# A list schedule that models the port of VectorE and GpSimd, with refitted durations and load queue

## The chip, the cores and the metric

The kernel runs on one core of one Trainium2 chip. The core has TensorE (matrix products, results in PSUM), VectorE, ScalarE and GpSimd (work on tiles in SBUF; VectorE and ScalarE also read PSUM) and SyncE, which issues the DMA transfers. In the profile these are PE, PEld (TensorE's weight loads), DVE, ACT, POOL and SP. The metric is device time in microseconds of one execution.

## The reference

Two layers of a block work on x of 1024 tokens by 1024 columns, in float32. Each layer normalises x, projects it to three mixers, joins their outputs, and runs a gated FFN of width 2816. The mixers are an attention over the 256 keys that an index score selects per query (`dsa`), a recurrent RWKV-7 mixer with eight heads, and an attention with compressed, selected and windowed keys (`nsa`).

```python
def reference(x, c, ...):
    for l in range(DEPTH):
        mod = jax.nn.silu(c) @ ada_w[l] + ada_b[l]
        sh1, sc1, g1, sh2, sc2, g2 = jnp.split(mod[:, None, :], 6, axis=-1)
        h = rms_norm(x, norm1_g[l]) * (1.0 + sc1) + sh1
        z = h @ w_in[l]
        za, zb, zc = split_cols(z, (sum(A_COLS), sum(B_COLS), sum(C_COLS)))
...
        mixed = jnp.concatenate([o_a, o_b, o_c], axis=-1) @ w_out[l]
        x = x + g1 * mixed
        h = rms_norm(x, norm2_g[l]) * (1.0 + sc2) + sh2
        gate, up = jnp.split(h @ ffn_wi[l], 2, axis=-1)
        x = x + g2 * ((jax.nn.silu(gate) * up) @ ffn_wo[l])
    return x
```

## The kernel before

Activations lie transposed, 128 features by 512 tokens, and the 1024 tokens are worked in two halves. A dense product (`dense`, output tile `mm`) splits weights and activations into a high and a low part and adds three products: high by high, high by low, low by high. Each weight tile of 128x512 (`wraw`) is loaded, its high part `whi` made by ScalarE and its low part `wlo` by GpSimd (`split`, called from `Feed.ahead`). `norm` and `rsqrt` make reciprocal roots with a chain of small VectorE instructions on 128x128 tiles (`nex` for the norms, `kex` for keys and queries, `ex` in RWKV, `rx`, `ru`, `ry` for narrow ones), then `cast` spreads them with matmuls (`rb`, `bc`). `attend` makes scores (`at`), masks and maxima on VectorE (`p`, `m`, `nb`), exponentials on ScalarE, scales `p` by `rs` on VectorE, transposes it on TensorE (`pt`), copies it with ScalarE (`pT`) and multiplies by the values (`po`). `topk` finds a threshold bit by bit: for each of 31 bits VectorE and ScalarE count (`junk`, `junka`, `tk_cn`), and three or four narrow VectorE instructions follow. `rw_unit` is the RWKV mixer of two heads (`am`, `A`, `TX`, `Tn`, `S`, `sh`, `sd`, `y`, `o`).

The order of all this is not written out by hand. It is made in three passes when the kernel is built.

1. `Weave.run` runs the generators of all streams (projections and FFN, attention, top-k, compression, RWKV, the modulation) in turns. It keeps a clock per engine from `cost_of` and `LAT` and takes the stream of best priority that is due and whose buffers fit. A first run finds how long each tile lives, a second one uses it. The result is a list of records (`Program.add`) with buffers given out; a record's number is its place in this list.
2. `Program.order` list-schedules the records. Each engine has a heap of records whose inputs are there. The engine that is free earliest takes its record of lowest number. It models TensorE as 4x4 cells so that narrow matmuls overlap, ScalarE's table loads, and loads as one wire of 390 GB/s that end 1.7 us after their bytes.
3. `Program.issue` emits the records sorted by their planned start. From there each engine's queue is in that order, and semaphores make it wait where an input is late.

Costs depend on the engine key (`PE`, `V`, `S`, `G`, `D` for loads), the operation and the width n. All instructions come out of one line of `issue`, so the profile shows L672 for nearly all; they are told apart by their tiles.

Of the kernel before, what the change touches and what calls it, by code (L numbers as in the profile page):

```python
# [18 lines left out]
AF = mybir.ActivationFunctionType  # L19
# [7 lines left out]
D = 1024  # L27
# [159 lines left out]
class Held:  # L187


    def __init__(self, weave, tag, key, make):  # L190
        self.weave, self.tag, self.key, self.make = weave, tag, key, make
        self.touches, self.end, self.got = 0, 0.0, None
# [8 lines left out]
    def __getattr__(self, name):  # L201
        return getattr(self.view(), name)
# [18 lines left out]
class Weave:  # L221
# [150 lines left out]
    def add(self, prio, gen, scope=None):  # L372
        c = self.cur
        c.children += 1
        self.live.append(Stream(prio, self.now(), len(self.live) + 1e-3, gen, scope or (c.scope, "child", c.children)))
# [37 lines left out]
    pass  # L413


LAT = {"PE": 0.17, "V": 0.1, "S": 0.1, "G": 0.1, "D": 0.0}


def cost_of(key, name, aps, kw):

    n = max(x.free_size() if callable(x.free_size) else x.free_size for x in aps[:2])
    psum = any(x.space == PSUM for x in aps[:3])
    acc = "accum_out" in kw
    if key == "V":
        if psum:
            return 0.1 + n / 860.0 + (0.1 if acc else 0.0)
        if name == "tensor_scalar":
            return 0.2 + n / 1250.0 + (0.2 if acc else 0.0)
        if name == "tensor_tensor_scan":
            return 1.25  # L430
        return 0.22 + n / 820.0
    if key == "S":
        return 0.18 + n / 1180.0 + (0.19 if acc else 0.0)
    if key == "G":
        return 0.12 + n / 417.0 if name == "tensor_tensor" else 0.1 + n / 1000.0
    a, b = aps[:2]
    plain = all(len(x.ap) <= 2 and x.ap[0][1] == 128 for x in (a, b))
    return 0.34 if plain else 0.59


class Timed:
# [5 lines left out]
    def __getattr__(self, name):  # L447
        f = getattr(self.eng, name)

        def call(*a, **k):  # L450
            a, k = [flat(x) for x in a], {n: flat(x) for n, x in k.items()}
            aps = [x for x in a + list(k.values()) if isinstance(x, bass.AP)]
            outs = [aps[0]] + ([k["accum_out"]] if "accum_out" in k else [])
            c = cost_of(self.key, name, aps, k)
            n = max(x.free_size() if callable(x.free_size) else x.free_size for x in aps[:2])
            self.weave.issue(self.key, 2.0 + n / 390.0 if self.key == "D" else c, aps, outs)
            if self.program is not None:
                self.program.add(self.key, name, a, k, aps, outs, c)
            else:
                f(*a, **k)  # L460

        return call
# [8 lines left out]


class Rec:
    __slots__ = ("key", "name", "a", "k", "cost", "deps", "n", "users", "pe", "func")


def spread(offset, dims, unit):
# [18 lines left out]
class Program:  # L496
# [29 lines left out]
            self.masks[key] = got  # L526
        return got

    def add(self, key, name, a, k, aps, outs, cost, pe=None):
        r = Rec()  # L530
        r.key, r.name, r.a, r.k, r.cost, r.pe = key, name, a, k, cost, pe
        r.n, r.deps, r.users = len(self.recs), set(), []
        r.func = a[2] if key == "S" and name == "activation" else None
        wrote = {id(x) for x in outs}
        for ap in aps:
            born = self.born.get(ap.tensor.name)
            if born is None:
                continue
            writes = id(ap) in wrote or (ap is aps[0])
            own = self.touched.setdefault(ap.tensor.name, ([], []))  # L540
            if born.pool == "ps":

                hit = False
                for e, w, eng in own[0]:
                    if w or writes:
                        r.deps.add(e)
                        hit = True
                if writes:
                    own[0].clear()
                if not hit and born.before is not None:  # L550
                    r.deps.update(born.before.recs)
                own[0].append((r.n, writes, key))
            else:
                p, m = self.region(ap, born)
                hit = False
# [12 lines left out]
                if writes:  # L568
                    assert not born.constant
                    own[0].append((r.n, p, m))  # L570
                elif born.pool != "const" or len(born.recs) < 400:
                    own[1].append((r.n, p, m))
                else:
                    born.constant = True
            born.recs.append(r.n)
        r.deps.discard(r.n)
        self.recs.append(r)

    def order(self):


        recs = self.recs
        missing = [len(r.deps) for r in recs]
        for r in recs:
            for d in r.deps:
                recs[d].users.append(r.n)
        free = {e: 0.0 for e in ("PE", "V", "S", "G", "D")}
        cells = [[0.0] * 4 for _ in range(4)]
        ready = {e: [] for e in free}
        coming = {e: [] for e in free}  # L590
        at = [0.0] * len(recs)
        wire, table = 0.0, None
        for r in recs:
            if not missing[r.n]:
                heapq.heappush(coming[r.key], (0.0, r.n))
        done, out = 0, []
        while done < len(recs):
            best = None
            for e in free:
                if ready[e]:  # L600
                    t = free[e]
                elif coming[e]:
                    t = max(free[e], coming[e][0][0])
                else:
                    continue
                if best is None or t < best[0]:
                    best = (t, e)
            t, e = best
            while coming[e] and coming[e][0][0] <= t:
                heapq.heappush(ready[e], heapq.heappop(coming[e])[1])  # L610
            n = heapq.heappop(ready[e])
            r = recs[n]
            if e == "PE":
                rows, cols, c = r.pe
                s = t
                for i in range(*rows):
                    for j in range(*cols):
                        s = max(s, cells[i][j])
                for i in range(*rows):
                    for j in range(*cols):  # L620
                        cells[i][j] = s + c
                free[e] = s + (c if rows[1] - rows[0] == 4 and cols[1] - cols[0] == 4 else 0.015)
                end = s + c
            elif e == "D":
                s = t
                free[e] = t + r.cost
                size = r.a[0].free_size() * r.a[0].partition_size() * 4
                wire = max(wire, free[e]) + size / 390e3
                end = wire + 1.7
            else:  # L630
                s, c = t, r.cost
                if r.func in (AF.Exp, AF.Silu) and r.func != table:
                    table, c = r.func, c + 1.28
                end = s + c
                free[e] = end - (0.05 if e == "V" else 0.02)
            out.append((s, n))
            done += 1
            for u in r.users:
                v = recs[u]
                at[u] = max(at[u], s + 0.001 if e == "PE" and v.key == "PE" else end + LAT[e])  # L640
                missing[u] -= 1
                if not missing[u]:
                    heapq.heappush(coming[v.key], (at[u], u))
        self.span = max(free.values())
        out.sort()
        return [recs[n] for _, n in out]

    def issue(self, tc, order, pools, inputs):
# [21 lines left out]
        with tc.manual_schedule():  # L670
            for r in order:
                getattr(engines[r.key], r.name)(*[real(x) for x in r.a], **{n: real(x) for n, x in r.k.items()})  # L672


def open_pools(ctx, tc):
# [1737 lines left out]
```

## Time and profile before

| | us |
|---|---|
| median of the runs shown | 3608.08 |
| lowest run | 3604.88 |
| the profiled execution's own time | 3599.41 |
| its span, first to last instruction | 3597.6 |
| mean granted clock of TensorE, share of full speed | 0.958 |

One run of the three shown took 11286.33 us; nothing here is compared with it. The profile page gives busy times of the whole span: PE 3318.0 us (92%), PEld 2503.0 (70%), DVE 2284.4 (63%), ACT 1820.8 (51%), POOL 1498.6 (42%). Busy is the time in which an engine executes at least one instruction; a busy VectorE or GpSimd instruction may be held up inside its own duration. `x232` counts instructions, `<-` stands between what is written and what is read.

### The profile page before, as it was taken

The page shows a single profiled execution, that of the slowest core. Times are in us where ns is not written, and L with a number is a line of the kernel's source. Part 1 is how long each engine was busy: PE and PEld are TensorE (multiplying, and loading weights), DVE is VectorE, ACT ScalarE, POOL GpSimd, SP SyncE. Part 2 cuts the span into 40 slices and gives each one's busy share as a digit, 9 for nine tenths or more (in the row PEclk, how much of TensorE's full clock was granted, in tenths as well). Part 3 has the DMA queues.
Part 4 walks back from the last instruction along what each step waited for, and adds up shares of the span by engine and source line. Part 5 has one row for each costly group of instructions (what it writes and reads, how often), then busy time and mean ns, then how long its engine had stood idle before and what let it go on. Part 6 is the DMA issues. An engine that isn't in the chain of part 4 may idle for free. (4 is left out here: it accounts for less than half of the span.)

```text
span 3597.6 us, 58814 instructions
## 1 busy us (share of the span) xinstructions
PE 3318.0 (92%) x20564; PEld 2503.0 (70%) x20564; DVE 2284.4 (63%) x5705; ACT 1820.8 (51%) x3724; POOL 1498.6 (42%) x1235
## 2 busy tenths in 40 slices
PE   7998999889899998989899998998999998689999
PEld 3756767657576776777677886776887775468887
DVE  4778889788978644798873115788774576442112
ACT  3545556646575554545555334567744545543222
POOL 3533434234423334552534554444554341035554
PEclk9999999889999999999999999999999999889999
DMA  8673445245622223553223333552332232023333
GB/s 278 212 250 110 141 130 183 56 125 171 195 61 79 75 94 124 156 161 114 76 68 108 97 97 109 168 175 97 98 108 82 79 106 66 27 66 92 97 97 98
DMA packets 354757, 425.01 MB, mean 118 GB/s; under 512 B 129686, under 2 KB 167190, under 8 KB 354460
## 3 DMA queue, kind: packets, MB, share of 16 engines
q1 hardware_dynamic: 354460, 421.25, 38.2%
q8 instruction: 162, 2.65, 0.3%
q14 instruction: 135, 1.11, 0.1%
HBM read 347.06 MB, written 60.44 MB: 113 GB/s over the span
## 5 line engine op out<-in xcount | busy, mean ns | idle before, releaser
L672 POOL TENSOR_TENSOR wlo<-wraw,whi 128x512 fp32r<-128x512 f32 (+1 forms) x808 | 1071.5, 1328 | 1469.4 <-ACT whi L672 1387.3
L672 ACT ACTIVATE whi<-wraw 128x512 fp32r<-128x512 f32 (+1 forms) x808 | 500.9, 621 | 900.5 <-PE mm L672 588.0
L672 PE MATMUL mm<-hh,whi 128*128 128x512 f32 x2144 | 868.0, 407 | 32.9 <-ACT hh L672 13.0
L672 PE MATMUL mm<-hl,whi 128*128 128x512 f32 x2112 | 846.5, 401 | 8.7 <-DVE hl L672 6.2
L672 PE MATMUL mm<-hh,wlo 128*128 128x512 f32 x2128 | 848.0, 399 | 6.1 <-POOL wlo L672 5.7
L672 PEld LDWEIGHTS mm<-hh,whi 128*128 128x128 f32 x2144 | 410.3, 192 | 146.1 <-issue 27.6
L672 PEld LDWEIGHTS mm<-hh,wlo 128*128 128x128 f32 x2128 | 407.9, 192 | 102.1 <-POOL wlo L672 12.4
L672 PEld LDWEIGHTS mm<-hl,whi 128*128 128x128 f32 x2112 | 405.1, 192 | 103.0 <-DVE hl L672 9.7
L672 DVE SCALAR_TENSOR_TENSOR x<-mm,mod,x 128x512 f32<-128x512 f32 x232 | 172.7, 747 | 255.9 <-PE mm L672 255.4
L672 DVE TENSOR_TENSOR sg<-sg,mm 128x512 f32<-128x512 f32 x87 | 59.5, 684 | 409.7 <-PE mm L672 407.2
L672 PE MATMUL mm<-acthi,whi 128*128 128x512 f32 x704 | 283.2, 407 | 15.8 <-DVE sg L672 8.9
L672 PE MATMUL mm<-actlo,whi 128*128 128x512 f32 x704 | 277.5, 395 | 1.6 <-POOL actlo L672 1.6
L672 PE MATMUL mm<-acthi,wlo 128*128 128x512 f32 x704 | 278.1, 395 | 0.7 <-POOL wlo L672 0.7
L672 ACT COPY pT<-pt 128x512 f32<-128x512 f32 (+2 forms) x220 | 123.8, 588 | 188.2 <-PE pt L672 160.0
L672 ACT ACTIVATE p<-p,nb,rst 128x512 f32<-128x512 f32 (+3 forms) x256 | 170.6, 667 | 71.8 <-DVE nb L672 65.1
L672 PE MATMUL pt<-c_ident,p 128*128 128x128 f32 x816 | 153.5, 312 | 55.1 <-DVE p L672 53.8
L672 PEld LDWEIGHTS pt<-c_ident,p 128*128 128x128 f32 x816 | 111.1, 158 | 103.5 <-DVE p L672 60.1
L672 ACT ACTIVATE junka<-score,tk_nt 128x512 int8<-128x512 f32 x240 | 165.8, 691 | 31.8 <-DVE tk_nt L672 28.1
L672 PEld LDWEIGHTS mm<-acthi,whi 128*128 128x128 f32 x704 | 133.5, 190 | 57.8 <-issue 11.6
L672 PEld LDWEIGHTS mm<-acthi,wlo 128*128 128x128 f32 x704 | 133.5, 190 | 29.8 <-POOL wlo L672 1.4
L672 PEld LDWEIGHTS mm<-actlo,whi 128*128 128x128 f32 x704 | 133.7, 190 | 28.0 <-POOL actlo L672 3.3
L672 DVE TENSOR_SCALAR p<-p,rs 128x512 f32<-128x512 f32 (+3 forms) x288 | 142.0, 560 | 0.6
(384 smaller groups left out, 6075.4 us busy)
## 6 DMA issues: line engine op xcount, KB each, us to landing
wraw<-in_wi_dram SPq DMA_DIRECT2D x352, 256.0 KB, 2.6
ada<-in_ada_dram SPq DMA_DIRECT2D x192, 256.0 KB, 4.6
wraw<-in_win_dram SPq DMA_DIRECT2D x184, 256.0 KB, 3.1
wraw<-in_wo_dram SPq DMA_DIRECT2D x160, 256.0 KB, 2.6
x<-x SPq DMA_DIRECT2D x64, 256.0 KB, 3.7
w<-in_w_dram SPq DMA_DIRECT2D x64, 256.0 KB, 3.6
wraw<-in_wout_dram SPq DMA_DIRECT2D x64, 256.0 KB, 2.6
o_in<-o SPq DMA_DIRECT2D x32, 256.0 KB, 3.2
```

What stands on the lines that cost most here:

```text
L672: getattr(engines[r.key], r.name)(*[real(x) for x in r.a], **{n: real(x) for n, x in r.k.items()})
```

## The change

The records, their operands, tiles and transfers stay the same in kind and number. What changes is the model behind the order.

`cost_of` gets new figures and a second result: whether the instruction uses the port that VectorE and GpSimd share. For VectorE that is so when nothing lies in PSUM, there is no accumulated output, and the operation is not a reduction, reciprocal or transpose (copies and scalar operations of more than one column count); for GpSimd always. `LAT`, the time from an end to a reader on another engine, changes; a reader on the same engine now comes 0.035 us after the end. `OVER` is how far the next instruction of an engine may begin ahead of the end of the one before. The state of the machine moves into a class `Chip`. There, a port instruction starts only when the port is free and holds it to its end; a change between whole-array and partial matmuls costs 0.05 or 0.08 us; and a load starts only after the eighth load before it has landed. `order` now compares planned starts, and where a port instruction would wait more than 0.1 us it looks among the next seven ready ones for one without the port that fits ahead of it. `Weave` uses the new `cost_of` and `LAT` too, but knows no port.

```diff
-LAT = {"PE": 0.17, "V": 0.1, "S": 0.1, "G": 0.1, "D": 0.0}
+LAT = {"PE": 0.21, "V": 0.05, "S": 0.06, "G": 0.06, "D": 0.0}
+OVER = {"V": 0.078, "S": 0.05, "G": 0.04}
 def cost_of(key, name, aps, kw):
...
     if key == "V":
-        if psum:
-            return 0.1 + n / 860.0 + (0.1 if acc else 0.0)
-        if name == "tensor_scalar":
-            return 0.2 + n / 1250.0 + (0.2 if acc else 0.0)
+        more = 0.055 if len(aps) - acc - (name in ("scalar_tensor_tensor", "tensor_tensor", "tensor_tensor_scan",
+                                                   "copy_predicated", "tensor_tensor_reduce")) > 2 else 0.0
+        if name in ("tensor_reduce", "reduce_max", "reciprocal", "transpose", "tensor_tensor_reduce"):
+            return 0.15 + n / 960.0 + (0.085 if acc else 0.0), False
+        if acc or psum:
+            return 0.15 + more + n / 960.0 + (0.085 if acc else 0.0), False
+        if name in ("tensor_scalar", "tensor_copy", "memset"):
+            return 0.15 + more + n / 1900.0, n > 1
         if name == "tensor_tensor_scan":
-            return 1.25
-        return 0.22 + n / 820.0
+            return 0.17 + n / 487.0, True
+        return 0.15 + more + n / 960.0, True
     if key == "S":
-        return 0.18 + n / 1180.0 + (0.19 if acc else 0.0)
+        return (0.16 if psum else 0.2) + n / 1200.0 + 0.09 * (len(aps) - 2), False
     if key == "G":
-        return 0.12 + n / 417.0 if name == "tensor_tensor" else 0.1 + n / 1000.0
+        if name == "tensor_tensor":
+            return 0.18 + n / (461.0 if all(x.ap[1][0] for x in aps[1:]) else 590.0), True
+        return 0.11 + n / 1220.0, True
...
-    return 0.34 if plain else 0.59
+    return 0.375 if plain else 0.63, False
...
+                n = ready[e][0]
+                s = max(chip.start(recs[n]), at[n])
+                if s > t + 0.1 and recs[n].port:
+
+                    for m in heapq.nsmallest(8, ready[e])[1:]:
+                        if not recs[m].port and t + recs[m].cost < s + 0.1:
+                            n, s = m, max(t, at[m])
+                            break
+                if best is None or s < best[0]:
+                    best = (s, e, n)
...
+class Chip:
...
+    def start(self, r):
+
+        t = self.free[r.key]
+        if r.key == "PE":
+            rows, cols, _ = r.pe
+            part = rows[1] - rows[0] + cols[1] - cols[0] < 8
+            for i in range(*rows):
+                t = max(t, max(self.cells[i][cols[0]:cols[1]]))
+            return t + (0.0 if part == self.part else 0.08 if part else 0.05)
+        if r.key == "D":
+            return max(t, self.ring[0])
+        return max(t, self.port) if r.port else t
...
+        if r.port:
+            self.port = s + c
+        self.free[r.key] = s + c - OVER[r.key]
+        return s + c
+
+    def after(self, r, u, s, end):
+
+        if r.key == u.key:
+            return s if r.key == "PE" else end + 0.035 if r.key != "D" else end
+        return end + LAT[r.key]
```

## Rows read from the trace of the kernel before

**Rows 1.** Stretches: length, busy us of PE, PEld, DVE, ACT, POOL; PEclk, DMA share, GB/s

```profile
0.00:90.00 90.00, 65.70 (x253) 35.37 (x254) 43.21 (x93) 33.80 (x59) 30.69 (x40) 0.91 0.85 278
90.00:1260.00 1170.00, 1079.65 (x7663) 777.18 (x7662) 961.00 (x2571) 670.02 (x1457) 455.50 (x378) 0.95 0.45 137
...
1440.00:1890.00 450.00, 416.59 (x3338) 319.20 (x3337) 372.82 (x987) 233.78 (x490) 202.68 (x164) 0.98 0.39 115
1890.00:2160.00 270.00, 266.56 (x1198) 215.25 (x1197) 59.24 (x100) 100.50 (x167) 135.20 (x109) 1.00 0.33 101
2160.00:2610.00 450.00, 411.50 (x1935) 320.83 (x1934) 333.00 (x825) 281.92 (x605) 210.43 (x166) 0.94 0.42 130
...
2970.00:3240.00 270.00, 215.61 (x1426) 152.52 (x1421) 141.96 (x411) 132.73 (x292) 50.02 (x43) 0.88 0.17 52
3240.00:3597.60 357.60, 350.94 (x1555) 288.40 (x1553) 68.34 (x89) 109.75 (x181) 178.88 (x142) 1.00 0.31 97
sum 3597.60, PE 3318.02 PEld 2502.97 DVE 2284.41 ACT 1820.83 POOL 1498.62; mean PE 368.67 PEld 278.11 DVE 253.82 ACT 202.31 POOL 166.51
```

**Rows 2.** Waits of TensorE: total us, times, longest us

```profile
PE pt L672 <- DVE p L672: 53.8, 31, 6.9
PE rb L672 <- DVE nex L672: 17.1, 3, 7.0
...
PE mm L672 <- ACT whi L672: 9.9, 5, 8.1
```

**Rows 3.** Durations by tile: ns shortest/median/longest

```profile
L672 DVE SCALAR_TENSOR_TENSOR ex<-ex x96: 274/291/1387, 195.8 to 2941.0; 128x128 f32<-128x128 f32 x96
...
L672 POOL MEMSET sd<- x32: 518/525/801, 305.3 to 3037.8; 128x512 f32 x32
```

**Rows 4.** Groups of VectorE by shape: count, busy us, mean ns, idle before

```profile
L672 DVE SCALAR_TENSOR_TENSOR ex<-ex 128x128 f32<-128x128 f32 x96 | 51.1, 532 | 0.1
...
L672 DVE TENSOR_TENSOR A<-am,c_msi 128x512 f32<-128x512 f32 x64 | 41.5, 680 | 13.8 <-PE am L672 11.5 <-PE po L672 2.1
...
L672 DVE SCALAR_TENSOR_TENSOR hl<-nt,mod,hh 128x512 fp32r<-128x512 f32 x32 | 32.1, 1004 | 3.7 <-ACT hh L672 2.6
```

**Rows 5.** Timeline of VectorE, then GpSimd, 748 to 762: start us, us

```profile
747.74 0.29 DVE L672 TENSOR_SCALAR ex<-ssk 128x128 f32<-128x128 f32 x1
...
749.60 1.27 DVE L672 SCALAR_TENSOR_TENSOR ru<-ru,ry 128x8 f32<-128x8 f32 x1
...
751.31 1.75 DVE L672 TENSOR_TENSOR y<-y,ry 128x512 f32<-128x512 f32 x1
...
754.86 1.25 DVE L672 SCALAR_TENSOR_TENSOR ex<-ex 128x128 f32<-128x128 f32 x1
...
756.70 0.80 DVE L672 TENSOR_TENSOR ex<-ex 128x128 f32<-128x128 f32 x1
...
758.03 0.77 DVE L672 SCALAR_TENSOR_TENSOR ex<-ex 128x128 f32<-128x128 f32 x1
...
749.56 1.28 POOL L672 TENSOR_TENSOR wlo<-wraw,whi 128x512 fp32r<-128x512 f32 x1 [3.21 <-ACT whi L672]
751.16 1.36 POOL L672 TENSOR_TENSOR wlo<-wraw,whi 128x512 fp32r<-128x512 f32 x1 [0.31 <-ACT whi L672]
754.67 1.30 POOL L672 TENSOR_TENSOR o<-o,f 128x512 f32<-128x512 f32 x1 [2.15 <-ACT o L672]
```

**Rows 6.** Timeline, VectorE and TensorE, 2485 to 2493: start us, us, idle

```profile
2485.99 0.29 DVE L672 TENSOR_SCALAR nex<-ss 128x128 f32<-128x128 f32 x1
...
2486.59 0.74 DVE L672 TENSOR_SCALAR_CACHE_REDUCE junk<-sel,tk_tr 128x512 int8<-128x512 bf16 x1
...
2492.72 0.58 PE L672 MATMUL rb<-nex,c_sel 128*128 128x128 f32 x1 [7.01 <-DVE nex L672]
```

**Rows 7.** Busy time in two neighbouring stretches of 90 us, columns as in rows 1

```profile
810.00:900.00 90.00, 85.75 (x647) 64.94 (x646) 80.47 (x182) 57.66 (x123) 36.14 (x26) 1.00 0.55 171
900.00:990.00 90.00, 75.25 (x399) 52.77 (x398) 84.97 (x173) 53.59 (x109) 43.22 (x33) 0.95 0.61 193
```

More of the change, by code (lines that the diff above doesn't have):

```diff
@@ L453, in call @@
             outs = [aps[0]] + ([k["accum_out"]] if "accum_out" in k else [])
-            c = cost_of(self.key, name, aps, k)
+            c, port = cost_of(self.key, name, aps, k)
             n = max(x.free_size() if callable(x.free_size) else x.free_size for x in aps[:2])
@@ L457, in call @@
             if self.program is not None:
-                self.program.add(self.key, name, a, k, aps, outs, c)
+                self.program.add(self.key, name, a, k, aps, outs, c, port=port)
             else:
@@ L473 @@
 class Rec:
-    __slots__ = ("key", "name", "a", "k", "cost", "deps", "n", "users", "pe", "func")
+    __slots__ = ("key", "name", "a", "k", "cost", "deps", "n", "users", "pe", "func", "port")
 def spread(offset, dims, unit):
@@ L527, in region, with add @@
         return got
-    def add(self, key, name, a, k, aps, outs, cost, pe=None):
+    def add(self, key, name, a, k, aps, outs, cost, pe=None, port=False):
         r = Rec()
-        r.key, r.name, r.a, r.k, r.cost, r.pe = key, name, a, k, cost, pe
+        r.key, r.name, r.a, r.k, r.cost, r.pe, r.port = key, name, a, k, cost, pe, port
         r.n, r.deps, r.users = len(self.recs), set(), []
@@ L579, in order @@
     def order(self):
-        recs = self.recs
+        recs, chip = self.recs, Chip()
         missing = [len(r.deps) for r in recs]
@@ L586, in order @@
                 recs[d].users.append(r.n)
[L587 to L590, printed above, removed]
+        ready = {e: [] for e in ENGINES}
+        coming = {e: [] for e in ENGINES}
         at = [0.0] * len(recs)
-        wire, table = 0.0, None
         for r in recs:
@@ L595, in order @@
                 heapq.heappush(coming[r.key], (0.0, r.n))
-        done, out = 0, []
-        while done < len(recs):
+        out = []
+        while len(out) < len(recs):
             best = None
[L599 to L629, printed above, removed]
-            else:
[L631 to L635, printed above, removed]
@@ new lines, in order @@
+            for e in ENGINES:
+                t = chip.free[e]
+                if not ready[e]:
+                    if not coming[e]:
+                        continue
+                    t = max(t, coming[e][0][0])
+                while coming[e] and coming[e][0][0] <= t:
+                    heapq.heappush(ready[e], heapq.heappop(coming[e])[1])
+                n = ready[e][0]
[7 more added lines that the diff above has]
+                    best = (s, e, n)
@@ L636, in order @@
+            s, e, n = best
+            if ready[e][0] == n:
+                heapq.heappop(ready[e])
+            else:
+                ready[e].remove(n)
+                heapq.heapify(ready[e])
+            end = chip.put(recs[n], s)
             out.append((s, n))
-            done += 1
-            for u in r.users:
+            for u in recs[n].users:
                 v = recs[u]
-                at[u] = max(at[u], s + 0.001 if e == "PE" and v.key == "PE" else end + LAT[e])
+                at[u] = max(at[u], chip.after(recs[n], v, s, end))
@@ L643, in order @@
                     heapq.heappush(coming[v.key], (at[u], u))
-        self.span = max(free.values())
+        self.span = max(chip.free.values())
+        self.starts = {n: s for s, n in out}
         out.sort()
@@ L672, in issue, with __init__, put @@
                 getattr(engines[r.key], r.name)(*[real(x) for x in r.a], **{n: real(x) for n, x in r.k.items()})
+ENGINES = ("PE", "V", "S", "G", "D")
+class Chip:
+    def __init__(self):
+        self.free = {e: 0.0 for e in ENGINES}
+        self.cells = [[0.0] * 4 for _ in range(4)]
+        self.part, self.port, self.wire, self.table, self.ring = False, 0.0, 0.0, None, [0.0] * 8
+    def start(self, r):
[9 more added lines that the diff above has]
+        return max(t, self.port) if r.port else t
+    def put(self, r, s):
+        if r.key == "PE":
+            rows, cols, c = r.pe
+            for i in range(*rows):
+                self.cells[i][cols[0]:cols[1]] = [s + c] * (cols[1] - cols[0])
+            self.part = rows[1] - rows[0] + cols[1] - cols[0] < 8
+            self.free["PE"] = s + (0.007 if self.part else c)
+            return s + c
+        if r.key == "D":
+            self.free["D"] = s + r.cost
+            size = r.a[0].free_size() * r.a[0].partition_size() * 4
+            self.wire = max(self.wire, s + r.cost) + size / 390e3
+            self.ring = self.ring[1:] + [self.wire + 1.5]
+            return self.wire + 1.5
+        c = r.cost
+        if r.func in (AF.Exp, AF.Silu) and r.func != self.table:
+            self.table, c = r.func, c + 1.28
+        if r.port:
+            self.port = s + c
+        self.free[r.key] = s + c - OVER[r.key]
+        return s + c
+    def after(self, r, u, s, end):
+        if r.key == u.key:
+            return s if r.key == "PE" else end + 0.035 if r.key != "D" else end
+        return end + LAT[r.key]
 def open_pools(ctx, tc):
```

## Prediction

> **What bounds the kernel now.** I read the busy time of each engine by stretch first, then TensorE's waits, then durations, and last the timeline of two places. TensorE is busy 3318.02 of 3597.60 us, so 279.6 us are idle, but not everywhere. In the two stretches of plain FFN work TensorE is busy 266.56 of 270.00 and 350.94 of 357.60 us with the clock at 1.00 [rows 1]; nothing is to be won there. Three stretches are different: in 90:1260, 1440:1890 and 2160:2610, where attention, top-k and RWKV run beside the projections, VectorE is busy 961.00, 372.82 and 333.00 us (82, 83 and 74%) and GpSimd 39 to 47%. I call them the contended stretches. TensorE idles 90.4 + 33.4 + 38.5 = 162 us in them, and the granted clock of 0.95, 0.98 and 0.94 [rows 1] says that some of the time ran at 1.2 instead of 2.4 GHz: 0.05 x 1170 + 0.02 x 450 + 0.06 x 450 = 94 us of full speed withheld. The rest of the idle time is the start (24 us), the tail of attention in 2970:3240 (54 us) and small pieces.
>
> TensorE's waits say who is late: the largest entry is the transposes `pt` waiting for VectorE's `p` (53.8 us, 31 times), then `rb` waiting for `nex` (17.1 us in 3 waits) [rows 2]. These are late results of VectorE. The reader should see why in the duration of one kind of instruction: the 128x128 links `ex` of the reciprocal-root chain have a median of 291 ns but a maximum of 1387 [rows 3], and a mean of 532 [rows 4]. The timeline shows where the microsecond comes from. `ru`, 8 columns wide, starts at 749.60, 0.04 us after GpSimd's 1.28 us `wlo`, and ends with it: 1.27 us. `y` takes 1.75 us across the next `wlo`, and an `ex` link 1.25 us beside GpSimd's `o` [rows 5]. VectorE's instructions that read or write PSUM do not show this: `A<-am` has a mean of 680 ns for 512 columns, while `hl`, of the same width and all in SBUF, has 1004 [rows 4].
>
> **The change part by part.** No instruction and no transfer is added or removed: the change alters only numbers by which the order of all recorded instructions is chosen, loads on SyncE's queue among them, and so the order in which five in-order queues hold them. What can be won or lost is waiting alone.
>
> *Durations of VectorE.* The old formula gives an `ex` link 0.22 + 128/820 = 0.376 us and adds 0.1 us before the next link; the new one 0.15 + 128/960 = 0.283 us and 0.035 us, against a median of 0.291 [rows 3]. For `hl` the old price is 0.844 and the new one 0.738 plus whatever GpSimd holds, against a mean of 1.004 [rows 4]. The old figures are too long for a free link and too short for a held one, so the old plan puts VectorE's results in the wrong places in both directions.
>
> *The port.* In the new plan an SBUF instruction of VectorE and one of GpSimd exclude each other, and when VectorE's next one would wait over 0.1 us, one of the next ready instructions that needs no port goes first if it fits. The port instruction behind it is then late by 0.1 us at most, which is the cost of the rule. How much of the lost time is due to this? In the chain of [rows 5] the links run from 747.74 to the end of the last held one at 758.80, 11.1 us. Taking the new formula's free durations, the five held instructions lose 1.27 - 0.16, 1.75 - 0.68, 1.25 - 0.28, 0.80 - 0.28 and 0.77 - 0.28, together 4.2 of 11.1 us, or 0.38. The counter-example is the longest wait for `nex`: TensorE stands 7.01 us before `rb` at 2492.72, while the links from 2485.99 on alternate with counting passes `junk` of 0.74 us [rows 6]. GpSimd holds nothing there, and the new rule, which still takes the lowest record number that is ready, does not reorder it. So the bounds of what goes away are nothing and all of the 162 us; between them I take 0.4, nearest to the first chain: 65 us of idle time. With it goes 0.4 of the 94 us of withheld clock, but this counts only while TensorE has work, 0.7 of the time (an estimate: it is busy 215.61 of 270.00 us, 0.80, in the stretch with the lowest clock [rows 1], and the withheld clock lies round its stops): 26 us. Both lie on the path, because TensorE's queue is in order and a stop of its head stops all of it.
>
> *The false holds.* The plan also charges the port for memsets of GpSimd. The 32 memsets of `sd` take 525 ns at the median and 801 at the most [rows 3], so they hardly wait for anyone; the plan can hold VectorE for 32 x 0.53 = 17 us without cause. Between 0 and 17 I take 12 us back, since in these stretches VectorE seldom has a free slot to spare. The Trainium skill, page SBUF — State Buffer, section SBUF: two separate sides, says the pair of ports is an exclusive lock held for the whole instruction, and that a VectorE instruction with two SBUF inputs meets it only against a GpSimd instruction that reads SBUF; by that rule a memset does not count, and the memset row agrees.
>
> *Loads.* The new queue model lets a load start only when the eighth before it has landed. In 0:90, where the DMA engines are 0.85 busy, TensorE idles 24.3 us [rows 1], and its longest wait for `whi` is 8.1 us [rows 2]. Bounds 0 and 24; I take 5, because most of that stretch is bytes and not order. In the contended stretches the DMA share is 0.39 to 0.45 [rows 1] and the loads lie under matmuls.
>
> *ScalarE, latencies, partial tiles.* ScalarE's new figures add 0.09 us for each extra operand; they move positions by tenths of a microsecond. The cover is matmul work that is ready; without it a wait for ScalarE (`whi` 9.9 us in all [rows 2]) stays as it is. I take nothing, either sign possible within 10 us.
>
> Sum on the profiled execution: 65 + 26 + 5 - 12 = 84 us, 3597.6 - 84 = 3513.6 us of span. The profiled run's own time is 1.8 us above its span and the median of the runs 8.7 us above that, so 3524 us.
>
> **The rivals.** *A: accurate but no better.* The plan now says when things happen, yet greedy order and record numbers stay, and stalls like that of [rows 6] and the tail's 54 us (GpSimd busy only 50.02 of 270.00 us there [rows 1]) remain. For it: no row shows that another VectorE instruction without the port was ready. Against it: VectorE mixes many streams in [rows 5]. Gain 0 to 45 us: about 3580.
> *B: more than forecast.* TensorE's busy time hides short waits, as its matmuls overlap. Its weight loads do not overlap so: they are busy 0.80 of the plain stretches and 0.66, 0.71 and 0.71 of the contended ones [rows 1]. At 0.80 the same loads would fill 777.18/0.80 = 971, 399 and 401 us of the 1170, 450 and 450, some 300 us less; part of that is only narrower tiles, so it is an upper end. If 0.6 of it goes, less 12 for the false holds, 168 us come off: 3440. The Trainium skill, page Trainium Kernel Development and Optimization, section Best Practices, calls matmul busy time a poor measure and wants the busy share of weight loads in its place; by that rule the sum's 91 us would be 0.4 x 300 = 120, and the time about 3495.
> *C: slower.* The first pass, which sets record numbers and buffer lives, uses the new prices without any port. A link costs it 0.283 + 0.05 instead of 0.376 + 0.1, while on the chip it takes 0.532. RWKV and top-k then look ready earlier, are woven in more tightly and hold PSUM banks while VectorE is behind. It decides where VectorE has no slack left: from 80.47 busy in 810:900 to 84.97 in 900:990 TensorE falls from 85.75 to 75.25 [rows 7]. If 8 of the 13 such slices in 90:1260 went that way, it would cost 8 x 10.5 = 84 us: about 3690. Against it: the second pass models the port and can hold these streams back.
> *D: no effect*, should the order hardly change: 3608. Nearly every price changes, so this only adds to A.
>
> **How the numbers follow.** Forecast (3485 to 3560) 0.45, A with D 0.30, B 0.13, C 0.12. The predicted time is 3524; its own range is 3485 to 3560. Within 2% of 3608 (about what a measurement of this kernel can tell from no change) means 3536 to 3680. Faster: two thirds of the forecast's chance, 0.30, B's 0.13, and 0.02 of A: 0.45. Slower: most of C, 0.09, and 0.01 of the others: 0.10. The rest, 0.45, is the same. The range goes from 3440, B's own value, to 3645, which takes in A, D and C's milder half.
>
> **What would show it.** Each step right: the mean of `ex` falls from 532 towards 400 ns; PSUM-reading instructions stand beside GpSimd's `wlo`; the wait of `pt` for `p` falls below 35 us; TensorE's idle time in the middle falls by some 60 us and the granted clock of 90:1260 rises above 0.95; the plain stretches stay as they are. Wrong: an unchanged mean of `ex` (the rule finds nothing to put in), a VectorE busy share over 0.9 for several slices on end (C), or long waits of TensorE that VectorE's port has no part in.

## The result: 3643.65 us, 1.0% slower

The median went from 3607.51 to 3643.65 us (four runs each). One of the four runs before, of 11286.33 us, is left out of the ratio, which is 1.0103, 95% interval 1.0064 to 1.0142. The time lies at the very top of the predicted range (3440 to 3645) and within 2%, but the sign is the opposite of the forecast's: 3524 us was forecast. The profiled execution of the changed kernel took 3654.92 us, its span 3653.1 us; the mean granted clock is 0.95, before it was 0.958.

The stretches of the changed kernel, columns as in [rows 1]:

```profile
0.00:90.00 90.00, 63.79 (x242) 32.30 (x242) 40.88 (x89) 30.05 (x54) 25.64 (x38) 0.87 0.82 270
90.00:1260.00 1170.00, 1056.56 (x7501) 761.00 (x7499) 918.96 (x2546) 648.87 (x1433) 428.11 (x365) 0.93 0.45 135
...
1440.00:1890.00 450.00, 382.00 (x2784) 289.07 (x2782) 337.10 (x913) 213.09 (x441) 181.64 (x147) 0.90 0.38 111
1890.00:2160.00 270.00, 267.99 (x1538) 212.82 (x1538) 80.40 (x196) 107.02 (x202) 125.78 (x108) 1.00 0.32 96
2160.00:2610.00 450.00, 408.02 (x2198) 311.86 (x2197) 270.06 (x676) 238.13 (x508) 187.58 (x155) 0.94 0.40 124
...
2970.00:3240.00 270.00, 259.11 (x1177) 200.37 (x1177) 84.47 (x167) 106.73 (x195) 111.32 (x89) 0.97 0.32 101
3240.00:3653.10 413.10, 402.75 (x1789) 327.45 (x1787) 98.14 (x139) 135.88 (x225) 201.54 (x159) 0.99 0.31 94
sum 3653.10, PE 3350.37 PEld 2513.23 DVE 2183.35 ACT 1790.21 POOL 1468.73; mean PE 372.26 PEld 279.25 DVE 242.59 ACT 198.91 POOL 163.19
```

TensorE idles 3653.10 - 3350.37 = 302.7 us, 23 more than before, and is busy for 32 us more with the same matmuls. In 90:1260 it idles 113 us (90 before) at a granted clock of 0.93 (0.95), and in 1440:1890 68 us (33) at 0.90 (0.98) [rows 1]. In these two stretches 7501 and 2784 matmuls were done, 7663 and 3338 before; what is left after 3240 us, mostly plain FFN work, takes 413.1 us in place of 357.6. VectorE, however, is busy 101 us less (2183.35 against 2284.41). That was the aim, and it came.

TensorE's waits and one group of VectorE by shape, after, as in [rows 2] and [rows 4]:

```profile
PE ssk L666 <- ACT dsq L666: 20.2, 7, 6.8
PE mm L666 <- DVE nt L666: 18.8, 7, 3.9
PE bc L666 <- DVE ex L666: 13.5, 3, 8.7
...
PE pt L666 <- DVE p L666: 11.0, 17, 1.6
```

```profile
L666 DVE SCALAR_TENSOR_TENSOR ex<-ex 128x128 f32<-128x128 f32 x96 | 40.3, 420 | 0.0
```

The mean of `ex` fell from 532 to 420 ns, and the wait of `pt` for `p` from 53.8 to 11.0 us. Both were named beforehand as signs that the forecast's mechanism works. They came, and still the kernel is slower. No single wait has taken the place of the old one: the new ones are many and small, for results of ScalarE and of VectorE. A loss of this kind comes from the order as a whole, and only runs can find its cause.

### The profile page after: what moved, and what is told of

Read it like the earlier page. It is cut to its first block, busy times and chain, and to the rows that moved or that the text cites. A ratio compares the mean times of both kernels' runs of the same rounds, so it can differ in the third digit from the quotient of the medians.

```text
span 3653.1 us, 58612 instructions
## 1 busy us (share of the span) xinstructions
PE 3350.4 (92%) x20564; PEld 2513.2 (69%) x20564; DVE 2183.3 (60%) x5705; ACT 1790.2 (49%) x3710; POOL 1468.7 (40%) x1235
## 5 line engine op out<-in xcount | busy, mean ns | idle before, releaser
L666 POOL TENSOR_TENSOR wlo<-wraw,whi 128x512 fp32r<-128x512 f32 (+1 forms) x808 | 1050.0, 1303 | 1494.3 <-ACT whi L666 1385.2
L666 PE MATMUL mm<-hh,whi 128*128 128x512 f32 x2144 | 880.3, 412 | 49.3 <-DVE nt L666 18.8
L666 PE MATMUL mm<-hh,wlo 128*128 128x512 f32 x2128 | 859.5, 405 | 3.1 <-POOL wlo L666 3.1
L666 PEld LDWEIGHTS mm<-hh,wlo 128*128 128x128 f32 x2128 | 413.1, 194 | 103.3 <-issue 10.4
L666 PE MATMUL pt<-c_ident,p 128*128 128x128 f32 x816 | 140.2, 286 | 17.1 <-DVE p L666 11.0
L666 PEld LDWEIGHTS pt<-c_ident,p 128*128 128x128 f32 x816 | 99.7, 144 | 59.2 <-DVE p L666 17.5
```

## The experiments

Each ratio is to the kernel before, which ran beside the experiment on the same chip, with its 95% interval; the time is the median. "New loop" is the changed `order` with its `Chip`, "old loop" that of before.

**Is it the new durations?** e1 gives `Weave` the old prices and leaves the new loop as it is. e2 is the converse, the old loop with the new prices in `Weave` alone. e5 is the old loop with the new durations and `LAT` in both passes. e6 is the new loop with the old durations, latencies and overlaps in the second pass.

```diff
 # e1, in the changed kernel: old formulas kept as weave_cost_of, LAT_WEAVE
-self.weave.issue(..., c, aps, outs)
+self.weave.issue(..., weave_cost_of(self.key, name, aps, k), aps, outs)
 # e5, in the kernel before, with the new cost_of
-LAT = {"PE": 0.17, "V": 0.1, "S": 0.1, "G": 0.1, "D": 0.0}
+LAT = {"PE": 0.21, "V": 0.05, "S": 0.06, "G": 0.06, "D": 0.0}
```

> The changed kernel, but the first pass (Weave) keeps the old prices and latencies, so record numbers and buffers are those of the kernel before; only the order pass is new. Theory W (the new prices in the first pass, which knows no port, spoil the record numbers): at most 1.000 times before, about 3590 us. Theory O (the order pass loses: the plan is exact and the chip does not follow it): 1.01 again, about 3640 us.

> The counterpart: the first pass uses the new prices and latencies, the order pass is that of the kernel before. Theory W: 1.01 to 1.02 times before, about 3650 us. Theory O: 1.00, about 3608 us.

> The order pass of the kernel before (one clock per engine, no port, no partial-tile charge, no limit on loads) with all the new prices and latencies, in both passes. e2 had the new prices in the first pass alone and was 0.994 times before. If the refitted durations and latencies harm the order pass because they leave no slack: 1.01 or more, 3640 us, and more waits of TensorE for VectorE and ScalarE than in e2. If the harm lies in the new machine (Chip and its choice by planned start): 0.99 to 1.00, about 3590 us.

> The counterpart of e5: the first pass as changed, the new machine with port, search, partial-tile charge and limit on loads, but the order pass has the old durations, latencies and overlaps. If the short new prices harm: 3590 us or less, since port and search then come on top of e2. If the machine harms: 3640 us or more.

Measured: e1 1.0272 (1.0249 to 1.0294), 3709 us; e2 0.9938 (0.9919 to 0.9956), 3587; e5 0.9899 (0.9863 to 0.9935), 3573; e6 1.0443 (1.0415 to 1.0471), 3770. The new durations are a gain in each of these runs: without them in `Weave` the changed kernel is 65 us slower still, and with them alone the kernel before gains 1.0% (e2's 0.6% is no more than the scatter found below). Rival C has its mechanism with the wrong sign. The loss is in the new loop.

e5 has no port in its plan, and yet two of the forecast's signs are there, first the wait of `pt`, then the mean of `ex`:

```profile
PE pt L680 <- DVE p L680: 19.3, 27, 1.9
```

```profile
L680 DVE SCALAR_TENSOR_TENSOR ex<-ex 128x128 f32<-128x128 f32 x96 | 44.9, 467 | 0.2
```

Of the fall of the wait from 53.8 to 11.0 us, and of the mean from 532 to 420 ns, more than half comes without any port. These signs do not tell the port from the new durations.

**Which part of the new loop?** Taken out or changed one at a time in the changed kernel: e3 the port (no record is marked), e4 the search for another ready instruction, e8 the charge for partial matmuls; e7 adds 0.2 us of slack in the plan to each result on its way to TensorE; e12 is e3 without the limit of eight loads.

```diff
 # e3                                  (in Program.add)
-r.port = ..., port
+r.port = ..., False
 # e4
-if s > t + 0.1 and recs[n].port:
+if False:
 # e7
-return end + LAT[r.key]
+return end + LAT[r.key] + (0.2 if u.key == "PE" and r.key in "VSG" else 0.0)
 # e8
-return t + (0.0 if part == self.part else 0.08 if part else 0.05)
+return t
 # e12, on top of e3
-return max(t, self.ring[0])
+return t
```

> The changed kernel with no instruction marked as using the port: new durations, latencies, partial-tile and load model, but VectorE and GpSimd do not exclude each other in the plan. If modelling the port helps and the rest of the refit hurts: slower than the changed kernel, 3680 to 3720 us, with the mean of the 96 ex links back at about 530 ns. If the port model itself does the harm: back to 3608 us or better.

> The changed kernel without the search among the next seven ready records for one that needs no port. If that search is what shortens VectorE's holds: VectorE's busy time goes back from 2183 towards 2284 us and the time goes up by 20 us or more, to 3665. If the search does the harm by moving records ahead of their number: 3610 to 3625 us.

> The changed kernel with 0.2 us more in the plan from the end of a VectorE, ScalarE or GpSimd instruction to a TensorE instruction that reads it; nothing else. If the plan is too exact, so that each late result stops TensorE's queue: faster than the changed kernel by 20 us or more, to 3620 or less, and less idle time of TensorE before partial matmuls. If slack is not what lacks: 3643 within 15 us.

> The changed kernel without the charge of 0.05 and 0.08 us for a change between whole-array and partial matmuls. The charge does not enter the choice among TensorE's records, only their planned times: if those times are right it helps, and without it the time is 3650 to 3670 us; if it harms, 3620 us.

> e3 (changed kernel without port, 3651 us) also without the limit of eight loads under way. If that limit delays loads and with them the split weights: 3600 to 3620 us. If it does nothing after the first 90 us: 3650 us within 10.

Measured: e3 1.0111 (1.0088 to 1.0134), 3651 us; e4 1.0187 (1.0162 to 1.0212), 3679; e7 1.0127 (1.0102 to 1.0153), 3657; e8 1.0227 (1.0193 to 1.0260), 3694; e12 1.0085 (1.0060 to 1.0110), 3642. The search and the charge each help within this loop, by 35 and 50 us. In e4 VectorE is busy 2206.7 us, little more than the 2183.35 of the changed kernel, so the search is not what shortened most of VectorE's holds. The whole port model together with its search is worth nothing (3644 against 3651): something eats its gain. Slack is not what the plan lacks, and the load queue matters by 9 us, less than the scatter found below.

**A fault in the choice.** In the new loop a record is moved to its engine's heap of ready ones whenever the engine is looked at, not only when the engine is chosen. From then on the engine counts as able to start at its free time, so a record of lower number that becomes ready a little later, but before the one in the heap can start, is not seen. e9 mends that; e10 is e9 without the port.

```diff
 # e9: a coming record is only looked at, and taken when its engine is chosen
-                if not ready[e]:
-                    if not coming[e]:
-                        continue
-                    t = max(t, coming[e][0][0])
                 while coming[e] and coming[e][0][0] <= t:
                     heapq.heappush(ready[e], heapq.heappop(coming[e])[1])
-                n = ready[e][0]
+                if not ready[e] and not coming[e]:
+                    continue
+                n = ready[e][0] if ready[e] else coming[e][0][1]
...
-            if ready[e][0] == n:
+            if not ready[e]:
+                heapq.heappop(coming[e])
+            elif ready[e][0] == n:
```

> The changed kernel with one fault of its choice mended: an engine with nothing ready looks at its next coming record without taking it into the ready heap, so a lower-numbered record that turns up earlier is not shut out until the first has run (in the plan of the changed kernel ScalarE passes over a ready lower number 101 times, in this one never). If this choice is the harm: 3600 us or less. If not: 3620 to 3660 us.

> The same with no instruction marked as using the port. Against e5 (old loop, same prices, 3573 us) only the machine's details are left: start of partial matmuls, limit on loads, same-engine latency. If the choice was the harm: 3570 to 3590 us. If the port costs what the mended choice gives: faster than e9. If the details harm: near 3650.

Measured: e9 1.0032 (1.0015 to 1.0048), 3621 us; e10 1.0021 (1.0006 to 1.0036), 3615. The mended loop is 23 us faster than that of the change with the port (e9) and 36 without it (e10 against e3). Still the port gains nothing.

**The port in the old loop, and how far orders scatter.** e11 is e5 with the port and the search put into the old loop. e15 is e5 with the charge for partial matmuls. e16 is e5 with 0.22 us in place of 0.21 us for `LAT["PE"]`, a change that should mean nothing.

```diff
 # e11, in the old loop; the search is put in as well
-                s, c = t, r.cost
+                s, c = max(t, port) if r.port else t, r.cost
...
+                if r.port:
+                    port = end
 # e15
-                s = t
+                s = t + (0.0 if p == part else 0.08 if p else 0.05)
+                part = p
 # e16
-LAT = {"PE": 0.21, ...
+LAT = {"PE": 0.22, ...
```

> e5 (old loop, all new prices, 0.990 times before) with the port and the search among the next seven ready records put into the old loop: a port record that is taken waits for the port inside the plan. If the port is worth modelling when the loop is sound: under 3573 us, about 3540. If modelling it makes the plan follow GpSimd too closely and stops help no one: 3590 us or more.

> e5 (old loop, all new durations, 3573 us) with one part of the new machine added: 0.08 us charged where TensorE goes from a whole matmul to a partial one and 0.05 us back. In the new machine this charge was worth 50 us (e8). If it is worth something in itself: 3530 to 3560, the fastest of all. If it only repairs something in the new loop: 3573 +/- 10. If the new machine's remaining loss of 42 us lies here: 3590 or more.

> e5 with one price changed by next to nothing: 0.22 us instead of 0.21 us from a matmul's end to its reader, in both passes. It sizes the scatter that any change of the order brings with it. If orders scatter by chance: off 3573 by 10 to 40 us in either direction, and differences of this size between the other runs carry no cause. If the time follows the prices smoothly: 3573 +/- 5.

Measured: e11 1.0075 (1.0048 to 1.0102), 3638 us; e15 0.9943 (0.9924 to 0.9962), 3589; e16 0.9950 (0.9934 to 0.9966), 3593. A hundredth of a microsecond in one price moves the median by 20 us; the two intervals barely touch. So a difference of some 20 us between two orders carries no cause by itself. The charge of e15 is not to be told from that; e11's 65 us over e5 (45 over e16) is. The port model, charged for both engines, does harm in a loop without the fault of the choice, too.

**Who waits for whom.** This led back to the trace. A place in the changed kernel, VectorE first, then GpSimd (start us, us):

```profile
346.10 0.28 DVE L666 TENSOR_TENSOR ex<-ex 128x128 f32<-128x128 f32 x1
346.30 0.68 DVE L666 TENSOR_TENSOR k<-k,f 128x512 f32<-128x512 f32 x1
346.90 0.28 DVE L666 SCALAR_TENSOR_TENSOR ex<-ex 128x128 f32<-128x128 f32 x1
347.10 1.22 DVE L666 SCALAR_TENSOR_TENSOR f<-r,vec,k 128x512 f32<-128x512 f32 x1
348.24 1.35 DVE L666 SCALAR_TENSOR_TENSOR ex<-ex 128x128 f32<-128x128 f32 x1
...
346.19 1.57 POOL L666 TENSOR_TENSOR qr<-r,lc 128x256 f32<-128x256 f32 x1 [4.64 <-ACT lc L666]
347.74 1.71 POOL L666 TENSOR_TENSOR o<-o,f 128x512 f32<-128x512 f32 x1
```

VectorE's `f` starts at 347.10, waits for `qr` to end at 347.76 and ends at 348.32. GpSimd's `o` starts at 347.74 and takes 1.71 us: it waits out the rest of `f`. VectorE's next instruction, `ex`, starts at 348.24 and takes 1.35 us, 1.07 over its free time of 0.28: it does not slip in ahead of `o` but waits for it. So `o` waits for what is left of one short VectorE instruction, while `ex` waits for what is left of a long GpSimd one.

It does not always go that way. `qr` itself, with a median of 772 ns, takes 1.57 us: while it stands, `ex` (346.10) and `k`, which began after it at 346.30, run at their free lengths of 0.28 and 0.68 us. The longest such case is in the kernel before, VectorE's line first, then GpSimd's:

```profile
1727.10 0.28 DVE L672 SCALAR_TENSOR_TENSOR nex<-nex 128x128 f32<-128x128 f32 x1
...
1725.39 3.11 POOL L672 TENSOR_TENSOR o<-o,f 128x512 f32<-128x512 f32 x1 [7.39 <-ACT o L672]
```

From 1725.48 to 1727.10 nine links of `ex` and `nex` begin, each 0.28 us long, before `o`, which takes 1.30 us in the median, gets its turn. A queue of short VectorE instructions can shut GpSimd out on the chip as well; the question is how often. The low weight parts of GpSimd in the changed kernel, by tile (ns shortest, median, longest) and by shape (busy us, mean ns):

```profile
L666 POOL TENSOR_TENSOR wlo<-wraw,whi x808: 725/1294/2181, 39.8 to 3640.0; 128x512 fp32r<-128x512 f32 x155, 128x256 fp32r<-128x256 f32 x7
...
L666 POOL TENSOR_TENSOR wlo<-wraw,whi 128x512 fp32r<-128x512 f32 x776 | 1025.4, 1324 | 1450.7 <-ACT whi L666 1347.0 <-PE mm L666 38.0 <-PE pt L666 15.7
```

The mean of `wlo` is 1324 ns at a median of 1294, 2% longer, and even the longest is 0.89 us over the median. `ex`, at 420 against 291 [rows 3], is 44% longer. The plan of the changed kernel says otherwise. Counted from that plan itself (planned start less the later of the engine's free time and the inputs' times), GpSimd's instructions wait 735 us for the port, in one case 10.15 us, nearly all of it for VectorE. VectorE's wait 494: 343 for GpSimd, and 150 for VectorE's own port instruction before. The latter is a second difference to the chip: `OVER` lets the next instruction begin 0.078 us ahead of the end of the one before, as `f` does at 347.10 while `ex` ends at 347.18, but the port is held to the end. To set the plan against the trace, take every instruction that lasts over 0.1 us longer than the median of its tile and shape, and add up what is over the median (an estimate of the holds): VectorE is held 347 us in the changed kernel, GpSimd 51. So the plan has VectorE's waits for GpSimd right and GpSimd's for VectorE many times too long.

While GpSimd's wait in the plan, VectorE starts 1853 port instructions in all. The reason is in the loop: when the port comes free both engines can start at the same time, the comparison `s < best[0]` keeps the first, and VectorE stands before GpSimd in `ENGINES`. A queue of short VectorE instructions thus shuts GpSimd out in the plan far more than on the chip. Low weight parts are then planned late, and the matmuls that read them too.

Four runs test this. e13 (in e9's loop), e14 (in e11's) and e17 (in the changed kernel, nothing else altered) let VectorE alone wait. e18 is e9 with GpSimd alone waiting.

```diff
 # e13, e17
-return max(t, self.port) if r.port else t
+return max(t, self.port) if r.port and r.key == "V" else t
...
-        if r.port:
+        if r.port and r.key == "G":
             self.port = s + c
 # e14: the same two conditions in the old loop, and the search for VectorE alone
 # e18: the same two lines as e13 with "G" and "V" exchanged
```

> The mended new loop of e9 (3621 us, 1.0032), with the port charged one way only: a VectorE instruction that uses the port waits until a GpSimd instruction that uses it has ended; a GpSimd instruction waits for nothing of VectorE. Theory O (the charge is wrong in one direction): in the trace of the changed kernel a GpSimd instruction of the 1.29 us form that starts while VectorE is within a port instruction lasts 1.29 to 1.33 us in the median, as long as alone, while the list schedule made its GpSimd wait; so the false waits put the low weight parts late and shift the streams. Then this runs at or under e10 (no port, 3615): 3575 to 3610. Theory N (a reorder by port is worth nothing here, in whichever direction it is charged): 3615 +/- 10. Theory H (holding VectorE back in the plan is what harms): 3620 or more.

> e11 (the old loop with all new durations, the port and the search, 3638 us, 1.0075) with the port charged one way only. e5, the same without port and search, took 3573. Theory O: most of the 65 us between e5 and e11 are the false waits of GpSimd: 3560 to 3590. Theory N or H: what VectorE's own wait does to the order is what costs: 3620 to 3645. If chance of the order alone makes tens of us (see e16), 3590 to 3620 tells nothing.

> The changed kernel (3644 us) with two lines altered: the port is charged one way only, a VectorE instruction waits for GpSimd's and never the other way round; the fault in the choice of the new loop stays. e13, with that fault mended, took 3509. Theory O (the false waits of GpSimd are what turned the gain around): at most e13 plus the 23 us that mending the fault was worth in e9, or somewhat more: 3520 to 3560, under the kernel before. If the fault in the choice is as much a cause as the direction: 3600 or more.

> e13's kernel (3509 us) with the port charged the other way only: a GpSimd instruction waits until VectorE's port instruction has ended, VectorE waits for nothing. Theory O: the false waits without the true ones: no better than no port at all (e10, 3615): 3610 to 3660. If any port charge spreads the two engines' work and so helps: 3510 to 3590.

Medians in us, with the ratio to the kernel before. In the column "both wait" VectorE also waits for its own port instruction before, in the others it does not:

| loop | no port | both wait | VectorE waits | GpSimd waits |
|---|---|---|---|---|
| of the change | 3651, 1.0111 (e3) | 3644, 1.0103 (the change) | 3557, 0.9859 (e17) | |
| mended | 3615, 1.0021 (e10) | 3621, 1.0032 (e9) | 3509, 0.9725 (e13) | 3635, 1.0071 (e18) |
| old, new durations | 3573, 0.9899 (e5) | 3638, 1.0075 (e11) | 3540, 0.9801 (e14) | |

The intervals are 0.9843 to 0.9875 (e17), 0.9702 to 0.9749 (e13), 0.9784 to 0.9819 (e14) and 1.0051 to 1.0092 (e18). In all three loops, letting VectorE's instructions hold the port as well costs 87 to 112 us, while VectorE's waits for GpSimd alone gain 94 and 106 us in the new loops and 33 in the old one (53 against e16). With nothing altered but the two lines that let VectorE's instructions hold the port, the changed kernel is 1.4% faster than the kernel before.

Which effect of those lines does the harm is not shown. They make GpSimd wait for VectorE, and they make VectorE wait for its own instruction before; no run has one without the other where VectorE waits for GpSimd. The loss does not follow the size of GpSimd's waits either. The old loop does not compare planned starts, so in e11's plan, counted in the same way, GpSimd waits 232 us in all and never more than 1.24, and still e11 is 98 us slower than e14; the changed kernel, with 735 us of such waits, is 87 slower than e17. And e18, whose plan has 302 us of GpSimd's waits and none of VectorE's, is only 20 us slower than e10, no more than the scatter. The fixed preference at a tie is thus not needed for the loss.

e13 is the fastest of all, 2.75% faster than before. One of its stretches with the sum, one wait of TensorE and one group of VectorE:

```profile
90.00:1260.00 1170.00, 1091.69 (x7821) 783.78 (x7820) 918.12 (x2639) 684.43 (x1500) 452.33 (x387) 0.96 0.46 140
...
sum 3501.90, PE 3295.55 PEld 2479.43 DVE 2155.02 ACT 1790.60 POOL 1481.10; mean PE 366.17 PEld 275.49 DVE 239.45 ACT 198.96 POOL 164.57
```

```profile
PE pt L666 <- DVE p L666: 6.2, 6, 3.7
```

```profile
L666 DVE SCALAR_TENSOR_TENSOR ex<-ex 128x128 f32<-128x128 f32 x96 | 43.9, 457 | 0.0
```

TensorE idles 206.4 us (279.6 before, 302.7 in the changed kernel) and is busy for 3295.55 us (3318.02, 3350.37). In 90:1260 GpSimd is busy 452.33 us, as before the change (455.50), where in the changed kernel it was 428.11: more of its work was done beside the other streams of this stretch. The mean of `ex` is 457 ns, longer than in the changed kernel, which is 134 us slower. How long VectorE is held tells little of the time; what the order puts in those places tells more.

## Why the prediction was wrong

*The step that failed* is the port. It was worked out from VectorE's side alone: how much of its lateness the rule takes away. "In the new plan an SBUF instruction of VectorE and one of GpSimd exclude each other" was taken as a true picture of the chip, and what the plan does with VectorE's instructions as holders of the port was not asked. So the bounds ran from nothing to all of 162 us, and a loss was left out without a reason. The runs showed that VectorE's waits for GpSimd are worth a gain, 94 us in this loop (e17 against e3), and that VectorE's instructions as holders cost 87 us of it (the change against e17) and 98 to 112 in the other loops. In the plan GpSimd waits 735 us, in the trace it is held some 51. [rows 5] had the hint: five VectorE instructions lost 4.2 us there, while the three of GpSimd took 1.28, 1.36 and 1.30 us. The code had two more: at a tie VectorE comes first, each time, and the port is held to the end of an instruction whose successor begins 0.078 us earlier.

*The size.* With the charge in the direction in which [rows 5] shows it (and the fault in the choice mended), the terms came nearly as they were priced: idle time fell by 73 us (65 forecast), busy time, which holds the clock's part, by 22 us (26 forecast), and the time is 3509 us (3524 forecast). That is the sum of the forecast for a kernel that this change was not. It is one order, and orders scatter by 20 us; the same charge is worth 106 us in this loop (e13 against e10) and 33 in the old one (e14 against e5). That 3509 lies so near to 3524 is in good part luck.

*The signs.* The mean of `ex` and the wait of `pt` came as forecast (420 ns, 11.0 us), while idle time and clock, named in the same list, went the other way (23 us more, 0.93 in 90:1260). The first two show that VectorE is held less, for which e5 needed no port (467 ns, 19.3 us); the latter show what the order did for the end. Signs at the bound engine should have been named first.

*The false holds of memsets* were priced at 12 us. No run tests it. The 32 memsets of `sd` take 520, 525 and 799 ns after, as in [rows 3].

*Loads.* 5 us of gain were taken; TensorE's idle time in 0:90 rose from 24.3 to 26.2 us, and without the limit of eight the time is 9 us less (e12 against e3, with intervals that overlap). Nothing was gained.

*ScalarE, latencies, partial tiles* were taken as nothing within 10 us. The durations and latencies together are worth a gain of 1.0% in the old loop (e5), or 0.5% in its twin e16. The charge for partial matmuls is worth 50 us in the changed kernel (e8) and no gain in the old loop (e15). The bound of 10 us was too narrow.

*The rivals.* A's 3580 missed the sign as well. C had the sign and not the mechanism: new prices in the first pass are a gain of 65 us (e1), and VectorE did not clog: in the two slices of [rows 7] it is busy 78.06 and 80.97 us in place of 80.47 and 84.97. B (3440) stayed out of reach for the best order too, and D fell with the first trace. Missing was the rival that the model itself is wrong for one of the two engines, with a price that could be counted beforehand: 735 us of GpSimd's waits in the plan.

*The rule of the Trainium skill* cited for the port (page SBUF — State Buffer, section SBUF: two separate sides) says that the instruction that starts first has the pair of ports for its whole length and the other blocks. The trace agrees where `o` waits for `f`, and `ex` for `o`. Where both are waiting, that section of the Trainium skill says nothing. The rows show both outcomes: GpSimd's `o`, begun at 347.74, went ahead of `ex`, begun at 348.24, but VectorE's `k`, begun at 346.30, went ahead of `qr`, begun at 346.19.

*What stays open:* what the 42 us between e10 and e5 are, two loops without port and with the same durations (20 of them may be scatter); and which of the two effects of the two lines costs the 87 to 112 us, GpSimd's waits for VectorE or VectorE's waits for its own instruction before. A two-way charge without the latter was not tried. That late low weight parts are the way by which the time is lost is argued from the plan and from GpSimd's busy time in 90:1260; the runs show only that the two lines are the cause.

## What to carry to other kernels

When a planner gets a model of a shared resource, ask for both users how long the plan makes each wait, and compare that with how much longer each one's instructions are in the trace; for GpSimd it was 735 us here against some 51. Look at what the planner does at a tie, and whether an engine comes to wait for its own last instruction. Charge the resource in one direction at a time before charging it in both. And before a difference between two list schedules is given a cause, move one price by next to nothing and see how far the time goes.

## What the hardware showed

In these traces the port costs VectorE much more than GpSimd: in the changed kernel some 347 us against some 51 (estimates from the durations, as above). GpSimd's `wlo` is held by 30 ns of 1294 in the mean and by 0.89 us at the most; an `ex` link of VectorE, 291 ns when free, takes up to 1375 ns. A GpSimd instruction that is waiting can get in ahead of VectorE's next one (347.74 and 348.24 above), and VectorE then loses most of a long GpSimd instruction. It can also be passed: `o` at 1725.39, before the change, took 3.11 us while nine links of 0.28 us went through. What decides between the two is not shown.
